# A decoder pair in three-pass float32r: the second pass of two heads' logits with 128 rows, and the lo pass of the probabilities with all 128 value columns

## The chip, the cores and the metric

The kernel runs on one core of one Trainium2 chip. A core has a matrix engine (TensorE; PE for its matmuls, PEld for its weight loads), a vector engine (DVE), a scalar engine (ACT), GpSimd (POOL) and a queue that issues most DMAs (SP). The metric is the device time of one execution in microseconds.

## The reference, cut to what matters

Two blocks over 512 tokens of width 1024. The first has two layers, each with four differential heads (two softmax maps of head dimension 64 are subtracted) and eight forgetting heads; the second has one layer with an mLSTM and an NSA mixer (eight query heads, two key groups, head dimension 64, a compressed, a selected and a window branch). With 512 tokens all eight key blocks are selected, so the selected and the window branch both work on all causal keys. The lines behind the change:

```python
# differential attention: two maps m of dimension 64 per head
logits = jnp.einsum('bqhmd,bkhmd->bhmqk', qi, k).astype(jnp.float32) * scale
p = jax.nn.softmax(logits, axis=-1)
p = p[:, :, 0] - lam * p[:, :, 1]
return jnp.einsum('bhqk,bkhe->bqhe', p.astype(v.dtype), v)
...
# NSA, selected and window branch
ls = jnp.einsum('bgrqd,bgqnd->bgrqn', qb, k_g).astype(jnp.float32) + bias_s
o_s = jnp.einsum('bgrqn,bgqnd->bgrqd', p_s, v_g.astype(jnp.float32))
```

## The kernel before

Every float32 operand x is split into hi (x rounded to float32r, by a copy) and lo = x - hi, and a product is made of three matmul passes, hi by hi, hi by lo and lo by hi (`mm3`, lines 165 to 169). Tokens lie in four tiles of 128.

For logits the head dimension is 64, half of the 128 rows of the array, so the three products are made in two passes. The query tile q holds hi of a map in one half of the partitions and lo in the other. The first pass multiplies it by a key tile that holds hi in both halves: 128 rows give hi·hi + lo·hi. The second pass takes only the 64 partitions of q that hold hi, and 64 partitions of a tile with the lo part of k: 64 rows give hi·lo. `logits` (line 551) issues both passes for each query tile i of a map m, with the first n = 128(i+1) keys as moving columns, so n is 128, 256, 384 and 512 equally often. The forgetting heads use line 551 as well, with two passes of 128 rows each, since their second tile carries the decay rows too (`fox_qk`).

For a differential head, `stacks` builds from the token-major projection a q tile (hi0, lo0, lo1, hi1, 64 columns each) and a k tile of 384 columns (hi0, hi0, lo0, lo1, hi1, hi1); `stack_T` transposes them by TensorE in groups of 128 columns (line 523, four transposes to a PSUM bank), and ACT or DVE (line 528) copies each bank to a `qk` tile. For NSA, `nsa_k` writes hi of a key group into both halves of `kn` and lo into partitions 0 to 63 (line 1518), and `nsa_soft` calls `logits`.

For the probabilities times values of forgetting and NSA heads, `pv_heads` transposes the probabilities (line 580), splits them into wh and wl, and issues for each pair of tiles a pass with the values as weights: 128 columns, hi in the first 64 and lo in the others, over wh (line 588), and a pass with the 64 hi columns over wl, into the upper 64 partitions of the sum (line 589). `fold` adds the two halves of the sum. The differential heads have their own `diff_pv`, with the weights from the probabilities.

The program interleaves a head's chain (logits, softmax, transposes, values) with matmuls of projections, gates and branches (the "feed"), which depend on weights from DMA. A scheduler with its own costs orders the instructions of each engine within these generators; the logits and stacks run under a higher priority (`hot`). PSUM has three banks with the tag A and five with the tag B; transposes and logits use B.

Of the kernel before, what the change touches and what calls it, by code (L numbers as in the profile page):

```python
# [10 lines left out]
F32 = mybir.dt.float32  # L11
F32R = mybir.dt.float32r
# [3 lines left out]
ALU = mybir.AluOpType  # L16
# [80 lines left out]
class Net:  # L97
# [410 lines left out]
        self.sub(v[:, 1:3, :], sq, v[:, 0:4:3, :])  # L508

    def k_stack(self, hl, sk):  # L510
        v = hl.rearrange("p (s d) -> p s d", d=64)
        kd = hl.rearrange("p (m c) -> p m c", c=128)[:, 0:3:2, :].rearrange("p m (e d) -> p m e d", d=64)
        self.copy(kd, sk[:, :, None, :].to_broadcast([128, 2, 2, 64]))
        self.sub(v[:, 2:4, :], sk, v[:, 0:6:5, :])

    def stack_T(self, tiles, bank='B'):

        out = []
        for which, cols in enumerate(((0, 128), (0, 256, 128))):
            for c in cols:  # L520
                p = self.pt(bank, F32R)
                for t in range(NT):
                    self.T.transpose(p[:, t * 128:(t + 1) * 128], tiles[which][t][:, c:c + 128], self.identr)  # L523
                if len(out) % 2 == 0:
                    two = self.t("qk", F32R, 1024 if len(out) < 4 else 512)
                o = two[:, len(out) % 2 * 512:len(out) % 2 * 512 + 512]
                if c == 128:
                    self.V.tensor_copy(o, p)
                else:
                    self.copy(o, p)  # L530
                out.append(o)
        q, k = out[:2], out[2:]
        return [((q[m], k[m]), (q[m][64 * m:64 * m + 64], k[2][64 * m:64 * m + 64])) for m in range(2)]

    def e_tile(self):

# [34 lines left out]
    def pv_heads(self, accs, es, val, packs, first, last):  # L571

        mm = self.T.matmul
        for pack in packs:
            p = self.pt("B")
            o, parts = 0, []
            for m, j in pack:
                n = 512 - 128 * j
                for i in range(j, NT):
                    self.T.transpose(p[:, o + (i - j) * 128:o + (i - j + 1) * 128], es[m, i][:, j * 128:(j + 1) * 128], self.ident)  # L580
                parts.append((m, j, slice(o, o + n)))
                o += n
            wh, wl = self.pair("pt")
            self.copy(wh[:, :o], p[:, :o])
            self.sub(wl[:, :o], p[:, :o], wh[:, :o])
            for m, j, c in parts:
                v, a = val(m, j), accs[m][:, j * 128:]
                mm(a, v, wh[:, c], start=first and j == 0, stop=False, skip_group_check=True)  # L588
                mm(a[0:64], v[:, 0:64], wl[:, c], start=False, stop=last and pack == packs[-1], skip_group_check=True)  # L589
            yield  # L590

    def fold(self, s, m, acc):
# [6 lines left out]
    def stage1(self, l, u):  # L599

        V = self.V
        unit = {}

        def start():
            unit["hls"] = [None] * NT, [None] * NT
            unit["rv"] = self.t("rw").rearrange("p (t m d) -> p t m d", t=NT, m=4)
            unit["vv"] = self.t("v", F32R)[:, :1024].rearrange("p (t s d) -> p t s d", t=NT, s=2)
            if u == 0:
                self.z = self.keep([128, NT, 8])

        def take(pair, ps):
            if pair == 0:
                start()
            with self.hot():
                take_hot(pair, ps)

        def take_hot(pair, ps):
            hls = unit["hls"]
            t0 = 2 * pair
            if pair == 0:  # L620
                v = self.t("hl", F32R)
                hls[0][:] = [v[:, t * 256:t * 256 + 256] for t in range(NT)]
            v = self.t("hl", F32R)
            hls[1][t0], hls[1][t0 + 1] = v[:, 0:384], v[:, 384:768]
            rv, vv = unit["rv"], unit["vv"]
            for t in (t0, t0 + 1):
                p = ps[t - t0]
                self.copy(rv[:, t], p[:, 0:256].rearrange("p (m d) -> p m d", m=4))
                self.copy(vv[:, t, 0, :], p[:, 256:384])
                self.sub(vv[:, t, 1, :], p[:, 256:384], vv[:, t, 0, :])  # L630
                if u == 0:
                    V.tensor_copy(self.z[:, t, :], p[:, 384:392])

            ts = slice(t0, t0 + 2)
            x = rv[:, ts, :, 0:16]
            ta, tb = self.t("r"), self.t("r")
            av = ta.rearrange("p (t m d) -> p t m d", t=2, m=4)
            bv = tb.rearrange("p (t m d) -> p t m d", t=2, m=4)
            cb = lambda z, lo, hi: z[:, ts, None, lo:hi].to_broadcast([128, 2, 4, hi - lo])
            V.tensor_tensor(av, x, cb(self.rc, 0, 16), op=ALU.mult)  # L640
            V.tensor_tensor(bv[:, :, :, 0:8], x[:, :, :, 8:16], cb(self.rs, 0, 8), op=ALU.mult)
            V.tensor_tensor(bv[:, :, :, 8:16], x[:, :, :, 0:8], cb(self.rs, 8, 16), op=ALU.mult)
            V.tensor_tensor(x, av, bv, op=ALU.add)
            for t in (t0, t0 + 1):
                self.stacks(hls, t, rv[:, t].rearrange("p m d -> p (m d)"))
        return take, unit
# [861 lines left out]
    def nsa_k(self, br, kv):  # L1508

        p = yield from self.dense_T(self.a["w_in_2"][0], (2824, 3080)[br])  # L1510
        b = self.bnk[:, br:br + 1]
        kv["ks"][br] = ks = []
        for g in range(2):
            own, other = slice(64 * g, 64 * g + 64), slice(64 - 64 * g, 128 - 64 * g)
            hi, lo = self.pair("kn")
            self.A(hi[own], p[own], AF.Identity, bias=b[own])
            self.A(hi[other], p[own], AF.Identity, bias=b[own])
            self.V.scalar_tensor_tensor(lo[0:64], p[own], b[own], hi[own].bitcast(F32), op0=ALU.add, op1=ALU.subtract)
            ks.append((hi, lo))
        yield  # L1520

# [60 lines left out]

    def nsa_soft(self, r, br, u, kv, es):
        hi, lo = kv["ks"][br][r // 2]
        qk = [((q, hi), (q[0:64], lo[0:64])) for q in u["q"]]
        for items in self.PACK:
            st, sc = self.t("s"), self.t("s")
            mine = [e for e, _ in self.logits(qk, items, u["bias"], rows=st)]
            n, gv = len(items), u["gv"][:, :, :, 1 + br]
            (m, i), last = items[0], items[-1]  # L1590
            g = gv[:, i, 0:2] if m != last[0] else gv[:, i:last[1] + 1:2, m] if n > 1 else gv[:, i:i + 1, m]
            self.V.reciprocal(sc[:, 0:n], st[:, 0:n])
            self.V.tensor_tensor(sc[:, 0:n], sc[:, 0:n], g, op=ALU.mult)
            for c, e in enumerate(mine):
                self.G.tensor_scalar(e, e, sc[:, c:c + 1], 0.0, op0=ALU.mult, op1=ALU.add)
                es[items[c]] = e
            yield
# [288 lines left out]
```

## Time and profile before

| | us |
|---|---|
| median of three runs | 2046.88 (2046.66 to 2047.39) |
| the profiled execution | 2052.8 |
| its span | 2050.8 |
| PE busy in it | 2007.6 (98%) |
| DVE busy | 1399.1 (68%) |
| ACT busy | 1070.7 (52%) |

The span of the profiled execution leaves out 2.0 us of that execution's time. Differential heads run at 50 to 165 us (first layer) and 650 to 770 us (second layer), NSA with the end of the mLSTM at 1420 to 1640 us. Starts of matmuls are recorded and their ends are modelled: a matmul's end lies past the start of the next, so what a matmul costs is read from start to start.

### The profile page before, as it was taken

The page shows a single profiled execution, that of the slowest core. Times are in us where ns is not written, and L with a number is a line of the kernel's source. Part 1 is how long each engine was busy: PE and PEld are TensorE (multiplying, and loading weights), DVE is VectorE, ACT ScalarE, POOL GpSimd, SP SyncE. Part 2 cuts the span into 40 slices and gives each one's busy share as a digit, 9 for nine tenths or more (in the row PEclk, how much of TensorE's full clock was granted, in tenths as well). Part 3 has the DMA queues.
Part 4 walks back from the last instruction along what each step waited for, and adds up shares of the span by engine and source line. Part 5 has one row for each costly group of instructions (what it writes and reads, how often), then busy time and mean ns, then how long its engine had stood idle before and what let it go on. Part 6 is the DMA issues. An engine that isn't in the chain of part 4 may idle for free.

```text
span 2050.8 us, 32727 instructions
## 1 busy us (share of the span) xinstructions
PE 2007.6 (98%) x12323; PEld 1770.9 (86%) x12323; DVE 1399.1 (68%) x2582; ACT 1070.7 (52%) x2129; POOL 635.2 (31%) x748
## 2 busy tenths in 40 slices
PE   8999989999999999999999999999999999999998
PEld 7988779999888988789999888888777689999987
DVE  5776778987426776778887427687665667788632
ACT  5666755554425666755554425456455535555521
POOL 0123336665201122344654201001111215565310
PEclk9999999999999999999999999999999999999999
DMA  5224242332423222342241423324221162323341
GB/s 147 73 65 121 90 161 83 124 120 78 164 78 104 74 76 78 119 136 98 87 144 62 164 84 118 110 77 124 72 73 43 51 216 73 124 83 104 113 154 52
DMA packets 198065, 211.03 MB, mean 103 GB/s; under 512 B 16263, under 2 KB 161257, under 8 KB 197907
## 3 DMA queue, kind: packets, MB, share of 16 engines
q1 hardware_dynamic: 190930, 183.24, 28.0%
q0 software_dynamic: 6976, 25.69, 3.3%
q8 instruction: 97, 1.59, 0.3%
q14 instruction: 62, 0.50, 0.1%
HBM read 196.30 MB, written 15.22 MB: 103 GB/s over the span
## 4 chain that ended last, share of the span: by engine, by line
PE 91%; DVE 3%; DMA 2%; ACT 2%; issue 1%; POOL 0%; SPq 0%; POOLq 0%; DVEq 0%; ACTq 0%
PE A L168 17%; PE A L167 17%; PE A L169 17%; PE B L168 10%; PE B L167 10%; PE B L169 10%; PE B L551 4%; PE B L580 1%; PE B L589 1%; PE B L588 1%; DMA raw<-in_w_in_dram 1%; PE B L717 1%; PE B L523 1%; DMA r<-in_w_up_dram 1%; PE B L703 0%
## 5 line engine op out<-in xcount | busy, mean ns | idle before, releaser
L163 DVE TENSOR_TENSOR lo<-raw,hi 128x1024 fp32r<-128x1024 f32 (+3 forms) x200 | 232.7, 1167 | 218.7 <-ACT hi L160 179.9
L160 ACT ACTIVATE hi<-raw 128x1024 fp32r<-128x1024 f32 (+4 forms) x208 | 204.5, 992 | 260.0 <-PE B L169 167.2
L163 DVE TENSOR_TENSOR lo<-r,hi 128x512 fp32r<-128x512 f32 (+1 forms) x240 | 269.5, 1155 | 47.3 <-ACT hi L160 42.3
L160 ACT ACTIVATE hi<-r 128x512 fp32r<-128x512 f32 (+1 forms) x240 | 193.6, 840 | 68.1 <-PE A L168 37.6
L167 PE MATMUL A<-store,hi 128*128 128x512 f32 (+1 forms) x624 | 220.0, 352 | 3.8 <-ACT hi L160 1.9
L168 PE MATMUL A<-store,hi 128*128 128x512 f32 (+1 forms) x624 | 219.3, 352 | 0.0
L169 PE MATMUL A<-store,lo 128*128 128x512 f32 (+1 forms) x624 | 218.2, 350 | 0.0
L168 PE MATMUL B<-store,hi 128*128 128x256 f32 x720 | 201.2, 279 | 0.0
L167 PE MATMUL B<-store,hi 128*128 128x256 f32 x720 | 201.2, 279 | 0.0
L169 PE MATMUL B<-store,lo 128*128 128x256 f32 x720 | 201.2, 279 | 0.0
L168 PE MATMUL A<-lo,store 128*128 128x512 f32 (+3 forms) x488 | 176.6, 363 | 0.8 <-DVE lo L163 0.8
L169 PE MATMUL A<-hi,store 128*128 128x512 f32 (+3 forms) x488 | 174.6, 361 | 2.2 <-DVE store L163 2.1
L167 PE MATMUL A<-hi,store 128*128 128x512 f32 (+3 forms) x488 | 173.2, 364 | 1.4 <-ACT store L160 1.1
L168 PEld LDWEIGHTS B<-store,hi 128*128 128x128 f32 x720 | 136.1, 189 | 0.1
L167 PEld LDWEIGHTS B<-store,hi 128*128 128x128 f32 x720 | 135.9, 189 | 0.1
L169 PEld LDWEIGHTS B<-store,lo 128*128 128x128 f32 x720 | 135.5, 188 | 0.0
L167 PEld LDWEIGHTS A<-store,hi 128*128 128x128 f32 x624 | 118.4, 190 | 19.5 <-ACT hi L160 2.4
L882 POOL TENSOR_TENSOR raw<-r,r 128x512 f32<-128x512 f32 x60 | 98.9, 1651 | 114.4 <-DMA r<-in_w_up_dram 81.4
L167 PE MATMUL A<-xs,hi 128*128 128x256 f32 x480 | 134.2, 280 | 0.0
L168 PE MATMUL A<-xs,hi 128*128 128x256 f32 x480 | 134.1, 279 | 0.0
L169 PE MATMUL A<-xs,lo 128*128 128x256 f32 x480 | 134.1, 279 | 0.0
L169 PEld LDWEIGHTS A<-store,lo 128*128 128x128 f32 x624 | 117.6, 188 | 14.4 <-issue 0.2
(427 smaller groups left out, 5572.2 us busy)
## 6 DMA issues: line engine op xcount, KB each, us to landing
r<-in_w_gate_dram SPq DMA_DIRECT2D x66, 512.0 KB, 4.5
r<-in_w_up_dram SPq DMA_DIRECT2D x66, 512.0 KB, 5.1
raw<-in_w_down_dram SPq DMA_DIRECT2D x66, 512.0 KB, 4.5
raw<-in_w_in_dram SPq DMA_DIRECT2D x64, 512.0 KB, 3.8
raw<-in_w_in_dram SPq DMA_DIRECT2D x104, 128.0 KB, 2.4
x_rows<-x POOLq DMA_DIRECT2D x20, 512.0 KB, 3.1
x<-x_rows POOLq DMA_DIRECT2D x20, 512.0 KB, 6.4
raw<-in_w_out_dram SPq DMA_DIRECT2D x28, 256.0 KB, 2.7
```

What stands on the lines that cost most here:

```text
L160: self.A(out, in_, AF.Copy, scale=scale)
L163: self.V.tensor_tensor(out, x, hi.bitcast(F32), op=ALU.subtract)
L167: mm(out, ah, bh, start=start, stop=False, skip_group_check=True)
L168: mm(out, ah, bl, start=False, stop=False, skip_group_check=True)
L169: mm(out, al, bh, start=False, stop=stop, skip_group_check=True)
L523: self.T.transpose(p[:, t * 128:(t + 1) * 128], tiles[which][t][:, c:c + 128], self.identr)
L551: self.T.matmul(pv, q[:, i * 128:(i + 1) * 128], k[:, :n], start=c == 0, stop=c == len(qk[m]) - 1, skip_group_check=True)
L580: self.T.transpose(p[:, o + (i - j) * 128:o + (i - j + 1) * 128], es[m, i][:, j * 128:(j + 1) * 128], self.ident)
L588: mm(a, v, wh[:, c], start=first and j == 0, stop=False, skip_group_check=True)
L589: mm(a[0:64], v[:, 0:64], wl[:, c], start=False, stop=last and pack == packs[-1], skip_group_check=True)
L717: mm(ov, wh[:, js], vv[:, j, :, :].rearrange("p s d -> p (s d)"), start=j == 0, stop=False, skip_group_check=True)
L882: G.tensor_tensor(s1, a21, a22, op=ALU.add)
```

## The change

`k_stack` builds a k tile of 512 columns (hi0, hi0, lo0, lo0, hi1, hi1, lo1, lo1), so that lo is there twice for each map; `stack_T` makes four groups of it instead of three. `nsa_k` writes lo into both halves. The second pass then takes the whole q tile and the whole lo tile: 128 rows, which adds lo·lo to the logits. The second pass over the probabilities takes all 128 value columns, into all 128 partitions of the sum, which adds lo·lo there.

```diff
     def k_stack(self, hl, sk):
-        v = hl.rearrange("p (s d) -> p s d", d=64)
-        kd = hl.rearrange("p (m c) -> p m c", c=128)[:, 0:3:2, :].rearrange("p m (e d) -> p m e d", d=64)
-        self.copy(kd, sk[:, :, None, :].to_broadcast([128, 2, 2, 64]))
-        self.sub(v[:, 2:4, :], sk, v[:, 0:6:5, :])
+        v = hl.rearrange("p (m z e d) -> p m z e d", m=2, z=2, d=64)
+        kk = sk[:, :, None, :].to_broadcast([128, 2, 2, 64])
+        self.copy(v[:, :, 0], kk)
+        self.sub(v[:, :, 1], kk, v[:, :, 0])
...
-        for which, cols in enumerate(((0, 128), (0, 256, 128))):
+        for which, cols in enumerate(((0, 128), (0, 256, 128, 384))):
...
-                    two = self.t("qk", F32R, 1024 if len(out) < 4 else 512)
+                    two = self.t("qk", F32R)
...
-                if c == 128:
+                if c in (128, 384):
                     self.V.tensor_copy(o, p)
...
-        return [((q[m], k[m]), (q[m][64 * m:64 * m + 64], k[2][64 * m:64 * m + 64])) for m in range(2)]
+        return [((q[m], k[m]), (q[m], k[2 + m])) for m in range(2)]
...
                 mm(a, v, wh[:, c], start=first and j == 0, stop=False, skip_group_check=True)
-                mm(a[0:64], v[:, 0:64], wl[:, c], start=False, stop=last and pack == packs[-1], skip_group_check=True)
+                mm(a, v, wl[:, c], start=False, stop=last and pack == packs[-1], skip_group_check=True)
...
-            hls[1][t0], hls[1][t0 + 1] = v[:, 0:384], v[:, 384:768]
+            hls[1][t0], hls[1][t0 + 1] = self.halves(v)
...
-            self.V.scalar_tensor_tensor(lo[0:64], p[own], b[own], hi[own].bitcast(F32), op0=ALU.add, op1=ALU.subtract)
+            for half in (own, other):
+                self.V.scalar_tensor_tensor(lo[half], p[own], b[own], hi[half].bitcast(F32), op0=ALU.add, op1=ALU.subtract)
...
-        qk = [((q, hi), (q[0:64], lo[0:64])) for q in u["q"]]
+        qk = [((q, hi), (q, lo)) for q in u["q"]]
```

The scheduler orders the instructions anew. First place: PE at the first differential head, from the last matmuls ahead of its logits. In the names, `qk_407` is the pair of q tiles, `qk_420` the two hi tiles of k, `qk_433` the lo tile (before) or the two lo tiles (after), and B_565, B_578 and so on are PSUM banks; a row with `qk_433` is a second pass. Before:

```order
L551 MATMUL B_578<-qk_420,qk_407 128x128
L551 MATMUL B_595<-qk_420,qk_407 128x384
L551 MATMUL B_595<-qk_433,qk_407 128x384
L551 MATMUL B_602<-qk_420,qk_407 128x384
L551 MATMUL B_602<-qk_433,qk_407 128x384
L551 MATMUL B_578<-qk_433,qk_407 128x128
L551 MATMUL B_623<-qk_420,qk_407 128x512
L551 MATMUL B_578<-qk_420,qk_407 128x256
L551 MATMUL B_623<-qk_433,qk_407 128x512
L551 MATMUL B_578<-qk_433,qk_407 128x256
```

And now, where B_584 is the bank of the second map that was B_578:

```order
L523 MATMUL B_435<-store_67,hl_310 128x128 x2
L523 MATMUL B_435<-store_67,hl_381 128x128 x2
L551 MATMUL B_571<-qk_420,qk_407 128x128
L551 MATMUL B_571<-qk_433,qk_407 128x128
L551 MATMUL B_571<-qk_420,qk_407 128x256
L551 MATMUL B_571<-qk_433,qk_407 128x256
L551 MATMUL B_584<-qk_420,qk_407 128x128
L551 MATMUL B_601<-qk_420,qk_407 128x384
L551 MATMUL B_601<-qk_433,qk_407 128x384
L551 MATMUL B_608<-qk_420,qk_407 128x384
L167 MATMUL A_545<-hi_464,store_67 128x384
L168 MATMUL A_545<-lo_465,store_67 128x384
```

The four transposes of the second map's lo tile (B_435) come right ahead of the logits; behind the last row shown stand 16 more projection matmuls of 384 columns, and only then the second map's second passes, with `B_608<-qk_433` first.

Second place: DVE at the same head, the copies from the transposes' banks to the `qk` tiles and what follows them. Before:

```order
L528 COPY qk_407<-B_409 128x512
L528 COPY qk_433<-B_428 128x512
L163 TENSOR_TENSOR v_518<-A_443,v_518 128x128
L640 TENSOR_TENSOR store_66<-rw_517,store_66 128x128
L641 TENSOR_TENSOR store_66<-rw_517,store_66 128x8x8
```

And now:

```order
L528 COPY qk_407<-B_409 128x512
L528 COPY qk_433<-B_428 128x512
L163 TENSOR_TENSOR v_524<-A_449,v_524 128x128
L528 COPY qk_433<-B_435 128x512
L640 TENSOR_TENSOR store_66<-rw_523,store_66 128x128
L641 TENSOR_TENSOR store_66<-rw_523,store_66 128x8x8
```

The second lo tile has a copy of its own, ahead of the rotary work of the next head and of the first softmax.

## Rows read from the trace of the kernel before

**Rows 1.** The page, busy time of PE and its share of the span:

```profile
PE 2007.6 (98%) x12323; PEld 1770.9 (86%) x12323; DVE 1399.1 (68%) x2582; ACT 1070.7 (52%) x2129; POOL 635.2 (31%) x748
```

**Rows 2.** The page, chain that ended last, by engine:

```profile
PE 91%; DVE 3%; DMA 2%; ACT 2%; issue 1%; POOL 0%; SPq 0%; POOLq 0%; DVEq 0%; ACTq 0%
```

**Rows 3.** Busy time by stage: stretch, its length, engines (instructions), PE clock, DMA:

```profile
50.00:165.00 115.00, 115.00 (x620) 97.80 (x620) 82.43 (x254) 73.20 (x201) 19.11 (x30) 1.00 0.22 61
...
1420.00:1640.00 220.00, 216.56 (x1038) 163.31 (x1037) 133.76 (x378) 114.65 (x256) 39.93 (x74) 1.00 0.19 61
```

**Rows 4.** Instructions of line 551, weight loads with two kinds of shapes (rows*columns):

```profile
L551 PEld LDWEIGHTS B<-qk,qk x128: 182/186/248, 50.5 to 770.1; 128*128 128x128 f32 x64, 64*128 64x128 f32 x64
...
L551 PEld LDWEIGHTS B<-kn,qk x128: 182/186/249, 1423.5 to 1627.9; 128*128 128x128 f32 x64, 64*128 64x128 f32 x64
```

**Rows 5.** Timeline of PE, differential head: start us, us, engine, line, tile, form:

```profile
57.44 0.82 PE L551 MATMUL B<-qk,qk 128*128 128x512 f32 x2
58.20 0.44 PE L168 MATMUL A<-lo,store 128*128 128x384 f32 x1
```

**Rows 6.** Timeline of PE, forgetting head, line 551 with two passes of 128 rows:

```profile
185.34 0.63 PE L551 MATMUL B<-hl,qk 128*128 128x512 f32 x2
185.80 0.22 PE L718 MATMUL B<-v,pt 128*128 128x128 f32 x1
...
192.69 0.44 PE L551 MATMUL B<-hl,qk 128*128 128x512 f32 x1
...
193.31 0.49 PE L703 MATMUL B<-store,ee 128*128 128x128 f32 x3
```

**Rows 7.** Timeline of PE, NSA: a pair between transposes, and four in a row:

```profile
1465.26 0.40 PE L551 MATMUL B<-kn,qk 128*128 128x512 f32 x1
...
1465.69 0.49 PE L551 MATMUL B<-kn,qk 64*128 64x512 f32 x1
1466.12 0.55 PE L580 MATMUL B<-store,ee 128*128 128x128 f32 x3
...
1494.23 1.21 PE L551 MATMUL B<-kn,qk 128*128 128x256 f32 x4
1495.38 0.39 PE L589 MATMUL B<-pt,vn 128*64 128x384 f32 x1
```

**Rows 8.** The chain that ended last, in order of time: transposes of the stacks:

```profile
71.27 0.81 PE B L523 x10
```

**Rows 9.** Timeline of PE, probabilities times values, 128 and 64 columns in turn:

```profile
1459.15 0.39 PE L588 MATMUL B<-pt,vn 128*128 128x512 f32 x1
1459.38 0.39 PE L589 MATMUL B<-pt,vn 128*64 128x512 f32 x1
1459.61 0.60 PE L580 MATMUL B<-store,ee 128*128 128x128 f32 x4
```

**Rows 10.** Groups of weight loads: busy us, mean ns of one, idle before:

```profile
L588 PEld LDWEIGHTS B<-pt,v 128*128 128x128 f32 x64 | 12.0, 188 | 9.3 <-ACT pt L160 7.9
L589 PEld LDWEIGHTS B<-pt,v 128*64 128x64 f32 x64 | 8.6, 135 | 3.6 <-DVE pt L163 2.4
```

**Rows 11.** Groups of DVE: copies of transposed stacks, subtractions, lo of NSA keys:

```profile
L528 DVE CAST qk<-B 128x512 fp32r<-128x512 f32 x16 | 10.7, 686 | 11.8 <-PE B L523 11.8
L163 DVE TENSOR_TENSOR hl<-rw,hl 128x128 fp32r<-128x128 f32 x64 | 16.1, 286 | 2.4 <-ACT hl L160 2.2
L163 DVE TENSOR_TENSOR vn<-cv,vn 128x256 fp32r<-128x256 f32 x4 | 1.7, 416 | 0.0
L1518 DVE SCALAR_TENSOR_TENSOR kn<-A,store,kn 64x512 fp32r<-64x512 f32 x4 | 3.0, 747 | 1.4 <-ACT kn L1517 1.4
```

**Rows 12.** Timeline of PE at the end of NSA, with the idle time before:

```profile
1603.76 1.21 PE L551 MATMUL B<-kn,qk 128*128 128x256 f32 x4
...
1627.02 1.32 PE L551 MATMUL B<-kn,qk 128*128 128x128 f32 x4
...
1638.05 0.96 PE L167 MATMUL A<-x,hi 128*128 128x512 f32 x3 [2.06 <-ACT x L160]
```

## The prediction

> **What bounds the kernel now.** I read the page's busy times first: PE is busy for 98% of the span [rows 1], and the chain that ended last is PE for 91% [rows 2]. An average can hide stages, so next come the stages that the change touches: in the first of the two differential stages PE is busy for all of 115 us (the second, 650 to 770 us, repeats it), in NSA for 216.6 of 220 us, while DVE stands at 82.4 of 115 us, 72%, and at 61% in NSA [rows 3]. The clock there is 1.00 throughout, the upper level of 2.4 GHz, so no time is to be had from it. The waits of PE in NSA hold one of any size, 2.06 us at the very end [rows 12]; in the two differential stages the view of PE's waits has no row at all. So these stages end when PE has worked off its list, and what PE does not do there comes off the end.
>
> But a busy PE is not a PE that streams at its peak, since ends of matmuls are modelled. I therefore read starts. Line 551 has 128 second passes with 64 rows, 64 in differential heads and 64 in NSA [rows 4], 32 of each of the four widths. In a differential head a first pass of 512 columns with 128 rows and a second one with 64 rows take from 57.44 to 58.20, 0.76 us, until the next matmul starts [rows 5]. The forgetting heads run the same line, the same two widths and the same sums with 128 rows in both passes, from 185.34 to 185.80, 0.46 us [rows 6]. The difference is 0.30 us for one second pass, and it is no wait for another engine: PE stands still on the way into the 64-row shape and again on the way out.
>
> **What the change takes away.** The same comparison at other places gives the bounds. Four NSA matmuls of 256 columns, two of them with 64 rows, take 1.15 us [rows 7]; the 1024 columns of the forgetting pair took 0.46 [rows 6]; that is 0.34 for each second pass, the upper end. Where transposes of the probabilities stand between the two passes, the NSA pair takes from 1465.26 to 1466.12, 0.86 us [rows 7], and a forgetting pair of the same width with a transpose between takes 0.62 [rows 6]: 0.24, the lower end. Transposes stand beside about a quarter of the second passes, so I take 0.29, near the clean pair. Where two second passes follow each other, as twice in the order of before shown above, the way in and out is paid once; there are nine such places, so 119 ways in and out. 119 x 0.29 = 34.5 us, with 119 x 0.24 = 28.6 and 119 x 0.34 = 40.5 as ends. About 8 us of it lie in each differential stage and 18 in NSA. A matmul of 64 rows and one of 128 stream the same columns, so the second pass itself grows by nothing.
>
> **What it adds on PE.** One more group of four transposes for each of eight differential units, 32 transposes. Ten in a row took 0.81 us [rows 8], so 32 x 0.081 = 2.6 us, all on the path, since PE has no idle time there. Between matmuls a transpose may cost more; at twice that it is 5.2.
>
> The second pass over the probabilities loads 128 columns of weights instead of 64. One load takes 188 ns instead of 135 [rows 10]. For 256 columns and more it runs beside the matmul ahead of it; for the 32 of 128 columns it does not quite fit, and I charge the whole difference: 32 x 0.053 = 1.7 us. The ends are 0 and, if none of the 128 were hidden, 6.8. Whether the change from 64 to 128 columns costs a standstill like that of the rows is read from the starts 1459.15, 1459.38 and 1459.61 [rows 9]: 0.23 us into and 0.23 out of the 64-column matmul, half of the forgetting pair's 0.46 each. So there is no standstill, and nothing is gained by dropping that shape.
>
> Sum on PE: 34.5 - 2.6 - 1.7 = 30 us less.
>
> **What it adds beside PE.** On DVE: eight copies of a bank at 0.69 us; 32 subtractions of 256 elements instead of 128, 0.42 against 0.29 us; four more lo halves of NSA keys at 0.75 us [rows 11]. That is 2.8 + 2.1 = 4.9 us in each differential stage and 3.0 in NSA. DVE then works some 87 of 107 us in the first stage, 82% instead of 72%, and 137 of 202 us in NSA, 68%: hidden by PE, which has no wait for DVE there now. If PE did wait for each of them, it would cost 12.8 us. The new order also puts in a wait: the second map's second passes wait for four transposes and a DVE copy that no other work needs. In PE's queue 18 projection matmuls of 384 columns stand ahead of them; at 0.46 x 384/1024 = 0.17 us each they cover 3.1 us, against 0.33 for the transposes and 0.69 for the copy. I cost it at nothing; without that cover each of the eight turns would cost about 1 us.
>
> What is late next: at the end of NSA, from 1603.76 to the group at 1627.02 us, 13 second passes save nearly 4 us [rows 12], but little other PE work is left there; the stage ends on logits, softmax, transposes and a wait for ACT of 2.06 us [rows 12]. I give back half, 2 us, and 1 us for short new waits in the stages, where PE now comes round sooner for what DVE and ACT make. Net 27 us less. The profiled execution took 2052.8 us, 5.9 more than the median of the runs shown; the change's part is the same in both within 0.1 us, so 2046.9 - 27 = 2020 us.
>
> **The rivals.** *DVE and ACT set the pace.* With DVE at 82% on average, bunches of copies and softmax steps may hold PE up; half of the 30 us comes back as waits: 2032 us. For it speaks that in NSA PE already waits at the end; against it that PE has no wait in the differential stages and that DVE's copies wait for PE's transposes, 11.8 us in all [rows 11].
>
> *The upper ends hold.* 0.34 us for each way in and out and no new waits: 40.5 - 4.3 = 36 us, 2011. The four NSA matmuls speak for it, the pairs between transposes against it.
>
> *The gap is not the rows.* If the 0.30 us came from a second pass as such, the change would take nothing away and its 4.3 us on PE would be added: 2051. Against it stand the forgetting heads, which have second passes and no gap. By the Trainium skill, "TensorE: Matmul & The Clock Gate", the table "Why this matters for your kernels", a single matmul of 32 rows takes the same time as one of 128, which read alone is this rival. By that rule, for the whole kernel, 2051; the trace disagrees with it for a 64-row matmul among 128-row ones, 0.76 against 0.46 us.
>
> *The columns stand still too.* If the ways into and out of the 64-column shape cost what the rows cost, hidden in both halves of that pair [rows 9], their 128 places would save another 128 x 0.29 = 37 us: 1983. The even 0.23 us speak against it. The Trainium skill, "TensorEngine Tiling (Array Packing)", "Key Properties", says that a change of tiling mode drains the engine, and lists 128 by 64 as a mode; for rows the trace agrees, for columns it shows no gap.
>
> *The turn becomes the wait* (the one that ends slower). PE runs its queue in order. If at each of the eight turns the copy of the fourth bank comes late behind DVE's queue, or its transposes wait for one of the five B banks, the second passes and all projections behind them stand. From 30/8 = 3.8 us for each turn the gain is gone; at 5 us it is 40 - 30 = 10 us more: 2057. Against it: the copy takes 0.69 us and 3.1 us of matmuls stand ahead.
>
> **How the numbers follow.** Forecast (2014 to 2026) 0.70; half comes back (2027 to 2038) 0.14; upper ends (2008 to 2013) 0.08; columns 0.02; not the rows 0.03; the turn 0.03. For 8 in 10 the range takes in the forecast, the upper ends to 2010 and the nearer part of the half: 2010 to 2033. About 0.2% (4 us) is what a measurement of this kernel can tell from no change. Faster by more than that: 0.70 + 0.14 + 0.08 + 0.02 = 0.94. Within it: a third of "not the rows", where the additions are partly hidden, and as much for a turn that just eats the gain, 0.02. Slower: 0.04.
>
> **What would show it.** Right: line 551 shows only 128 rows, a differential pair of 512 columns takes 0.46 us from start to start, four of 256 some 0.5; the differential stages are shorter by about 7 us each, NSA by 14 to 16, the rest stays. The forecast is wrong if line 551's starts still show 0.7 us and more, if PE shows waits for line 528 or for softmax that add up to over 10 us, or if a stage that has no second passes of 64 rows changes by more than a few us.

## The result and the profile after

The changed kernel takes 2014.2 us (median of 4 runs, 2006.1 to 2019.9), the kernel before on the same chip 2047.1 us (4 runs, 2046.7 to 2050.2). The ratio is 0.9833 with a 95% interval of 0.9814 to 0.9852: 33 us less. The forecast was 2020 us with 27 us less, in a range of 2010 to 2033. Direction and range hold; the saving is larger than the sum made it. In the two profiled executions the difference is larger still, 2012.6 us against 2052.8, 40.2 us; the last section says what is known of the 7 us between these two numbers.

The page of the kernel after: busy time and share of each engine, and the chain that ended last, by engine.

```profile
span 2010.7 us, 32817 instructions
...
PE 1970.4 (98%) x12355; PEld 1774.8 (88%) x12355; DVE 1396.6 (69%) x2594; ACT 1072.1 (53%) x2129; POOL 642.6 (32%) x748
...
PE 92%; DVE 3%; ACT 2%; DMA 2%; issue 1%; POOL 0%; SPq 0%; POOLq 0%; DVEq 0%; ACTq 0%
```

PE is busy for the same 98% of a span that is 40 us shorter, with 32 more instructions, the transposes [rows 1, 2]. So the share of busy time says nothing of the gain: the standstill was counted as busy time, since the ends of matmuls are modelled.

Two stages of the kernel after by windows (stretch, its length, busy time and instructions of PE, PEld, DVE, ACT and POOL, PE clock, DMA share, GB/s):

```profile
50.00:165.00 115.00, 115.00 (x677) 104.51 (x676) 93.41 (x281) 77.86 (x211) 21.70 (x32) 1.00 0.26 71
1420.00:1640.00 220.00, 216.80 (x1110) 179.56 (x1109) 151.56 (x366) 118.59 (x240) 44.24 (x84) 0.99 0.29 94
```

In the same 115 us PE starts 677 matmuls instead of 620, in NSA's 220 us 1110 instead of 1038 [rows 3]. (Work of the next stage has moved into the window, so the counts are not of the same work.) DVE stands at 81% in the differential stage, as forecast.

Line 551 of the kernel after (number of instructions: shortest, median, longest ns, first and last start, shapes as rows*columns), weight loads and matmuls, and the idle time of PE ahead of the line by what ended it:

```profile
L551 PEld LDWEIGHTS B<-qk,qk x128: 186/188/216, 49.3 to 758.4; 128*128 128x128 f32 x128
...
L551 PEld LDWEIGHTS B<-kn,qk x128: 186/188/212, 1404.5 to 1587.5; 128*128 128x128 f32 x128
L551 PE MATMUL B<-kn,qk x128: 218/340/482, 1404.6 to 1587.7; 128*128 128x512 f32 x32, 128*128 128x128 f32 x32, 128*128 128x384 f32 x32, 128*128 128x256 f32 x32
...
its engine sat idle before it (us, times) until:
...
  issue: 0.5, 1
```

All 256 loads of the changed heads have 128 rows where half had 64 [rows 4]. The last line is one that I had not read before predicting. "issue" is idle time for which the profile shows nothing that was waited for, and here it is idle time of the weight loads (PEld): for the matmuls of line 551 alone the view has no such line. It is 0.5 us once in the whole program, where the kernel before had

```profile
  issue: 20.8, 94
```

that is 94 places of 0.22 us. By the trace, 79 of the 94 stand ahead of a 64-row load behind a 128-row one and 14 ahead of a 128-row load behind a 64-row one; the last is the one that the kernel after still has. At the pair of [rows 5] it looks like this (PEld before, the idle time in brackets, and then PEld after at the pair that the next timeline shows):

```profile
57.77 0.18 PEld L551 LDWEIGHTS B<-qk,qk 64*128 64x128 f32 x1 [0.31 <-issue]
58.20 0.19 PEld L168 LDWEIGHTS A<-lo,store 128*128 128x128 f32 x1 [0.25 <-issue]
...
55.05 0.19 PEld L168 LDWEIGHTS A<-lo,store 128*128 128x128 f32 x1
55.28 0.19 PEld L169 LDWEIGHTS A<-hi,store 128*128 128x128 f32 x1
```

After, the load for line 168 starts at 55.05, 0.23 us ahead of its matmul at 55.28. Before, it starts at 58.20, together with its matmul [rows 5], and so does the 64-row load (57.77). It is so everywhere in the kernel before: at all 119 places where PE goes into the 64-row shape, and at all 119 where it comes out, the load starts within 0.003 us of its own matmul, while between two matmuls of 128 rows it starts 0.115 us ahead in the median. So where the number of rows changes, the load does not run ahead of its matmul. Whether that is the cause of the standstill or a sign of it, no run here shows.

The timeline of PE after, at the places that answer to [rows 5] and [rows 7]: start us, us, engine, line, operation, tile, shape.

```profile
54.82 0.63 PE L551 MATMUL B<-qk,qk 128*128 128x512 f32 x2
55.28 0.34 PE L168 MATMUL A<-lo,store 128*128 128x384 f32 x1
...
1584.16 0.64 PE L551 MATMUL B<-kn,qk 128*128 128x256 f32 x4
1584.63 0.34 PE L589 MATMUL B<-pt,vn 128*128 128x384 f32 x1
```

The differential pair of 512 columns takes 0.46 us instead of 0.76, and four NSA matmuls of 256 columns take 0.47 instead of 1.15: both are now what the forgetting heads took all along [rows 6].

Where the time went, from the starts of single matmuls in the two profiles (us; a stage runs from the first matmul of line 551 to the last one of its forgetting heads, NSA to the first matmul of the next feed-forward block):

| stretch | before | after | difference |
|---|---|---|---|
| first differential and forgetting stage | 189.8 | 181.9 | -7.9 |
| second | 188.1 | 180.0 | -8.1 |
| NSA to the next feed-forward block | 310.1 | 289.0 | -21.1 |
| ahead of the first stage | 50.7 | 49.3 | -1.4 |
| second feed-forward products to NSA's first line 551 | 291.3 | 289.8 | -1.5 |
| products of the first feed-forward block | 193.0 | 199.6 | +6.6 |
| products of the second | 199.6 | 193.0 | -6.6 |

The three stages hold 37 us. The two feed-forward blocks trade places; no line of theirs is changed.

### The profile page after: what moved, and what is told of

It reads as the page before. It is cut to its first block, busy times and chain, and to the rows that moved or that the text cites. A ratio compares the mean times of both kernels' runs of the same rounds, so it can differ in the third digit from the quotient of the medians.

```text
span 2010.7 us, 32817 instructions
## 1 busy us (share of the span) xinstructions
PE 1970.4 (98%) x12355; PEld 1774.8 (88%) x12355; DVE 1396.6 (69%) x2594; ACT 1072.1 (53%) x2129; POOL 642.6 (32%) x748
## 4 chain that ended last, share of the span: by engine, by line
PE 92%; DVE 3%; ACT 2%; DMA 2%; issue 1%; POOL 0%; SPq 0%; POOLq 0%; DVEq 0%; ACTq 0%
PE A L168 17%; PE A L167 17%; PE A L169 17%; PE B L169 10%; PE B L168 10%; PE B L167 10%; PE B L551 3%; PE B L580 1%; DMA r<-in_w_up_dram 1%; PE B L589 1%; PE B L523 1%; PE B L588 1%; PE B L717 1%; DVE lo L163 0%; PE B L703 0%
## 5 line engine op out<-in xcount | busy, mean ns | idle before, releaser
L883 POOL TENSOR_TENSOR r<-raw,r 128x512 f32<-128x512 f32 x60 | 98.6, 1645 | 113.8 <-DVE lo L163 106.9
```

Source lines behind the costliest of these rows:

```text
L883: G.tensor_tensor(a11, s1, a11, op=ALU.subtract)
```

## The experiments

The ratios are to the kernel before on the same chip: 2047.6 us (19 runs) for rows64, diff_only, nsa_only and pv_only, 2046.2 (15 runs) for after_again, grouped and three, 2045.4 (8 runs) for turned. "Ways" are the places at which PE comes to a 64-row second pass of line 551 from another shape, counted in the order of the trace; the kernel before has 119.

### rows64: the change with the second passes back at 64 rows

```diff
-        return [((q[m], k[m]), (q[m], k[2 + m])) for m in range(2)]
+        return [((q[m], k[m]), (q[m][64 * m:64 * m + 64], k[2 + m][64 * m:64 * m + 64])) for m in range(2)]
...
-        qk = [((q, hi), (q, lo)) for q in u["q"]]
+        qk = [((q, hi), (q[0:64], lo[0:64])) for q in u["q"]]
```

> The changed kernel with one thing undone: the second pass of the logits takes 64 partitions again (q hi and one half of the doubled lo tile); the fourth group of transposes, its copy, the doubled lo of the NSA keys and the 128 value columns stay. Theory (PE stands still on each way into and out of the 64-row shape, about 0.3 us for both): all of the gain goes and the additions stay, so 2047 + 3 = 2050 us, the first differential stage with the forgetting heads behind it about 190 us instead of 182, NSA up to the next feed-forward block about 310 instead of 289. Rival (the gain comes from the new order and from lo tiles that are made differently, not from the rows): stays near 2014 us, with 182 and 289 us.

Measured: 2053.3 us (10 runs, 2046.5 to 2062.7), ratio 1.0028 [1.0005, 1.005]. The whole gain is gone, and what the change adds is left, 6 us by the medians; by the stages the two differential ones are 2.9 and 2.3 us longer than before and NSA is 1.6 us shorter. The pair of 512 columns in its timeline (columns as above):

```profile
57.34 0.82 PE L551 MATMUL B<-qk,qk 128*128 128x512 f32 x2
58.10 0.44 PE L168 MATMUL A<-lo,store 128*128 128x384 f32 x1
```

It takes 0.76 us again, and the idle time of the weight loads ahead of line 551 is back:

```profile
  issue: 21.1, 93
```

All the additions are still in this kernel, and its 12,355 matmuls have the lines, tiles and widths of those of the kernel after, in the same order. Only the rows differ. So the rows carry the gain, and neither the order nor the new lo tiles do. Its stages are 192.7, 190.4 and 308.5 us against 181.9, 180.0 and 289.0 after: 40.8 us for 123 ways, 0.33 each.

### diff_only and nsa_only: the change in one kind of head

The first is the kernel before with the parts of the diff in the functions that build, transpose and pair the stacks (lines 510 to 533 and 624); the second has these two:

```diff
-            self.V.scalar_tensor_tensor(lo[0:64], p[own], b[own], hi[own].bitcast(F32), op0=ALU.add, op1=ALU.subtract)
+            for half in (own, other):
+                self.V.scalar_tensor_tensor(lo[half], p[own], b[own], hi[half].bitcast(F32), op0=ALU.add, op1=ALU.subtract)
...
-        qk = [((q, hi), (q[0:64], lo[0:64])) for q in u["q"]]
+        qk = [((q, hi), (q, lo)) for q in u["q"]]
```

> The kernel before with the differential part alone: k tile of 512 columns, four groups of transposes, second pass with 128 rows; NSA and the probabilities as before. Theory: the two differential stages get shorter by 8 us each as in the changed kernel (line 551 by 7.5 us each, the gaps ahead of it by 1, transposes longer by 1), NSA keeps its 310 us; about 16 us less, 2031. Rival (DVE's 4.9 us per stage and the wait for the fourth bank eat part): under 5 us for each stage, 2040.

Measured: 2026.7 us (2024.1 to 2034.5), ratio 0.9896 [0.987, 0.9922]. The differential stages are 8.2 and 8.4 us shorter, NSA 1.6 us longer. With the 1.6 us of added transposes that fall within these stages, 16.6 us net are 18.2 for 56 ways, 0.33 each.

> The kernel before with the NSA logits alone: lo of the keys in both halves, second pass with 128 rows; differential heads and probabilities as before. Theory: NSA up to the next feed-forward block goes from 310 to 289 us, the differential stages stay; about 21 us less, 2026. Rival (the end of NSA gives half back and part of the 21 us came from a luckier order): 14 us or less, 2033 or more.

Measured: 2029.0 us (2018.9 to 2032.2), ratio 0.9892 [0.9862, 0.9923]. From its first to its last matmul of line 551 and on to the next block NSA takes 287.6 us instead of 310.1: 22.5 us for 63 ways, 0.36 each. What PE waited for in NSA of this kernel (engine, line, releaser: us in total, times, longest):

```profile
PE A L167 <- ACT x L160: 2.1, 1, 2.1
PE B L1499 <- issue: 0.9, 1, 0.9
PE B L588 <- ACT pt L160: 0.5, 1, 0.5
PE B L580 <- POOL ee L1596: 0.5, 2, 0.3
PE B L1625 <- ACT wc L160: 0.3, 1, 0.3
PE B L589 <- DVE pt L163: 0.3, 1, 0.3
```

The wait at the very end was there before [rows 12]; the others come to 2.5 us, against 22.5 saved. In the stages that they change, the two halves save 16.6 + 22.5 = 39 us, of which the kernel after keeps 37 together with the 128-column pass. They are not quite separate: the differential stages, which were expected to stay, are 1.5 us longer each in nsa_only, as NSA is by 1.6 in diff_only and by 1.7 in pv_only. These kernels have new orders, so a change of 1 to 2 us in a single stage need not come from the rows.

### pv_only: the probabilities' lo part with 128 columns, alone

```diff
-                mm(a[0:64], v[:, 0:64], wl[:, c], start=False, stop=last and pack == packs[-1], skip_group_check=True)
+                mm(a, v, wl[:, c], start=False, stop=last and pack == packs[-1], skip_group_check=True)
```

> The kernel before with the lo pass of the probabilities alone: 128 value columns instead of 64. Theory (columns cost no standstill; only the longer weight load shows, where the matmul has 128 columns): 0.7 to 1.7 us more in all, 2048; line 589 up by some 0.02 us per matmul on average. Rival (a change of columns stands still as a change of rows does): some 0.29 us less for each of 128 places, 37 us less, 2010.

Measured: 2045.1 us (10 runs, 2040.0 to 2054.2), ratio 0.9993 [0.9973, 1.0014]: no difference, and the 0.7 to 1.7 us that were expected are too small for this ratio to show. Counted by starts, line 589 takes 1.4 us more in all, 0.9 of it in NSA. The timeline of PE in NSA, wide and narrow:

```profile
1457.34 0.40 PE L588 MATMUL B<-pt,vn 128*128 128x512 f32 x1
1457.58 0.39 PE L589 MATMUL B<-pt,vn 128*128 128x512 f32 x1
1457.81 0.27 PE L580 MATMUL B<-store,ee 128*128 128x128 f32 x1
```

0.24 and 0.23 us from start to start with 128 columns, 0.23 and 0.23 with 64 [rows 9]. A shape of fewer columns costs no standstill here; the rival of 1983 us falls.

### after_again: the kernel after once more

It is the changed kernel, run again to tell 33 us from 40.

> The changed kernel again, unaltered, to see how single executions of it and of the kernel before are spread. Theory: the stages of the change save 40 us in every execution (differential 8 + 8, NSA 21, rest), and what differs between executions is the pace of the 256-column matmuls in the first two feed-forward blocks, 113 or 118 ns, 7 us for a block; so the medians of many runs on one chip differ by 37 to 41 us (some 2008 against 2047), ratio 0.980 to 0.982. Rival (the change itself costs the feed-forward blocks time, and 33 us is what it is worth): a median of 2013 to 2015, ratio 0.983 to 0.985, and slow blocks in most profiles.

Measured: 2009.0 us (5 runs, 2003.5 to 2015.1), ratio 0.9828 [0.9805, 0.985], 37 us less. That is in agreement with the stages, but the interval of the ratio touches both expectations, so the ratio alone does not decide. The profile speaks against the rival: the stages are 181.9, 180.0 and 290.2 us, 36 us shorter than before, and slow blocks in most profiles, the rival's condition, are not there. Here the first block turned slow only near 455 us and the second stayed fast; in the first profile of this kernel the first block was slow and the second fast. Two profiles are few.

### grouped: both first passes of a group ahead of both second passes

The kernel before, with the loops of line 551 exchanged:

```diff
-            for c, (q, k) in enumerate(qk[m]):
-                self.T.matmul(pv, q[:, i * 128:(i + 1) * 128], k[:, :n], start=c == 0, stop=c == len(qk[m]) - 1, skip_group_check=True)
...
+        for c in range(2):
+            for _, pv, m, i in out:
+                q, k = qk[m][c]
+                self.T.matmul(pv, q[:, i * 128:(i + 1) * 128], k[:, :128 * (i + 1)], start=c == 0, stop=c == 1, skip_group_check=True)
```

This kernel does not compute what the reference does: where two logits share a bank, their two sums are interleaved in it, and the result is another. How that comes about no run here shows. The matmuls are the same in number, shape and operands.

> The kernel before, rows and all, with one thing altered: in a group of two logits both first passes are issued ahead of both second passes. The work is the same, but second passes of 64 rows can follow each other. Theory (the price is paid for each way into and out of the shape, not for each matmul): with 20 to 30 ways fewer, 6 to 9 us less, most in NSA (5 of it), about 2040; line 551 with its neighbours shorter by 0.3 us for each way that goes. Rival (each 64-row matmul costs 0.3 us by itself): no change beyond 2 us.

Measured: 2038.8 us (10 runs, 2033.7 to 2041.5), ratio 0.996 [0.9947, 0.9974], 7.4 us less. The order has 94 ways, 25 fewer: 0.30 each. No second pass has gone and none has more rows; only their neighbours have changed.

### turned: the passes of every second logit the other way round

The kernel before, with the order 128, 64, 64, 128 rows within a group in place of 128, 64, 128, 64; the sums are those of the reference.

```diff
-            for c, (q, k) in enumerate(qk[m]):
+            for c, (q, k) in enumerate(qk[m][::-1] if o and qk[m][1][0].shape[0] == 64 else qk[m]):
```

> The kernel before, with its 64-row second passes, where in a group of two logits the second one has its passes turned round: first 128 rows, then 64; then 64, then 128. No work is added or left out, and the sums are the same. Theory (a price for each way into and out of the shape): the two 64-row passes of a group stand side by side, some 25 to 35 ways fewer than 119, so 7 to 11 us less: about 2038, ratio 0.9945 to 0.9965. Rival (each 64-row matmul costs 0.3 us by itself): within 2 us of before, ratio 0.999 to 1.001.

Measured: 2037.5 us (5 runs, 2035.6 to 2039.2), ratio 0.9957 [0.9942, 0.9972]. 93 ways, 26 fewer: 7.9 us by the medians, 0.30 each. The stages are 1.1, 1.2 and 5.9 us shorter, 8.2 us, 0.31 each. The timeline of PE in NSA, a group of four and a single pair:

```profile
1484.82 1.02 PE L551 MATMUL B<-kn,qk 128*128 128x256 f32 x4
1485.68 0.34 PE L589 MATMUL B<-pt,vn 128*64 128x384 f32 x1
...
1486.94 0.83 PE L551 MATMUL B<-kn,qk 128*128 128x512 f32 x2
1487.70 0.66 PE L580 MATMUL B<-store,ee 128*128 128x128 f32 x4
```

Four of 256 columns with two 64-row passes side by side take 0.86 us: 1.15 when they stand apart [rows 7], 0.47 when no pass has 64 rows. The single pair, which has no neighbour to share with, still takes 0.76. Two 64-row matmuls in a row pay once, 0.39 us here with the matmul behind them inside the stretch. So the cost belongs to the change of shape and not to the 64-row matmul as such.

### three: fewer additions for the same rows

If only the rows matter, the fourth bank of the differential heads isn't needed. This kernel keeps the three transposed groups of the kernel before, whose third holds the lo parts of both maps' keys above each other, and uses all its 128 rows for either map; NSA is as in the kernel after, line 589 as before. Against the kernel after:

```diff
-        for which, cols in enumerate(((0, 128), (0, 256, 128, 384))):
+        for which, cols in enumerate(((0, 128), (0, 256, 128))):
...
-        return [((q[m], k[m]), (q[m], k[2 + m])) for m in range(2)]
+        return [((q[m], k[m]), (q[m], k[2])) for m in range(2)]
...
-                mm(a, v, wl[:, c], start=False, stop=last and pack == packs[-1], skip_group_check=True)
+                mm(a[0:64], v[:, 0:64], wl[:, c], start=False, stop=last and pack == packs[-1], skip_group_check=True)
```

The added half multiplies the lo part of a map's queries with the lo part of the other map's keys, a product of two lo parts that the reference does not have; the kernel after adds that of its own keys there, and the kernel before neither.

> 128 rows without the extra work: NSA as in the changed kernel, but for differential heads the k tile of 384 columns and three groups as before, where the second pass takes the whole q tile (hi and lo of one map) over the whole lo tile (lo of both maps), so that a product of lo by lo of the other map is added in place of the map's own; the probabilities' lo pass keeps its 64 columns. Theory: line 551 as in the changed kernel, 32 transposes fewer (2.2 us less on PE), the shorter weight load back (0.8 us less): 3 us below the changed kernel, ratio to before 0.979 to 0.981; first differential stage with the forgetting heads behind it 180.5 us instead of 182. Rival (the standstill comes back wherever the two halves of a tile hold different maps, or the fourth group cost nothing): differential stage 190 us, or no difference to the changed kernel.

Measured: 2000.3 us (5 runs, 1999.1 to 2001.4), ratio 0.9785 [0.9768, 0.9802], 46 us less than before and faster than both kernels: 8.7 us below after_again on the same chip, where 3 were expected. Its stages are 179.8, 178.2 and 287.7 us, 5.3 us less than those of the kernel after: 1.6 from line 523, 1.2 from line 589, 1.2 from line 551, the rest spread over the projections. Against the profile of after_again (spans of 1997.4 and 2006.9 us) the stages hold 6.4 us, the pace of the first block 1.5, and the stretches from the forgetting heads to the first two blocks 4.5, while 2.7 go back between the second block and NSA. Why those stretches differ is open. The matmuls of its first differential stage have the shapes of the kernel after:

```profile
L551 PE MATMUL B<-qk,qk x64: 218/334/477, 48.0 to 146.8; 128*128 128x128 f32 x16, 128*128 128x256 f32 x16, 128*128 128x384 f32 x16, 128*128 128x512 f32 x16
```

## Why the prediction was right, and where its sum was too small

**What bounds the kernel.** Right: what PE does not do came off the end. The three stages became 37 us shorter, and the chain is still PE's.

**The gap is the rows.** Right, and shown from three sides: rows64 takes the whole gain away by the rows alone, turned and grouped take a fifth to a quarter of it by order alone, and the pair fell from 0.76 to 0.46 us. The rival of 2051 falls. The Trainium skill, "TensorE: Matmul & The Clock Gate", the table "Why this matters for your kernels", gives a single matmul of 32 rows the time of one of 128; for 64 rows among 128 the runs show some 0.3 us beside it for every way in and out. The Trainium skill, "TensorEngine Tiling (Array Packing)", "Key Properties", says that a change of tiling mode drains the engine: for rows the runs agree, for columns (pv_only) they show no gap.

**0.29 us for a way in and out.** This term was mis-sized. The runs give 0.30 to 0.31 (turned, grouped), 0.33 (rows64, diff_only) and 0.36 (nsa_only). The last has 2.1 us of line 588 in it, which became 1.5 to 2.1 us shorter in NSA in rows64, diff_only and pv_only too, where NSA's second passes still have 64 rows, so that goes with the new order; without it nsa_only gives 0.32. For 119 ways 0.30 to 0.33 are 36 to 39 us instead of 34.5.

The step that failed is where the windows of [rows 5] and [rows 7] end: at the start of the matmul behind the second pass. That matmul is held up as well. In the timeline of PE it takes until the next start, before and then after:

```profile
58.20 0.44 PE L168 MATMUL A<-lo,store 128*128 128x384 f32 x1
58.48 0.34 PE L169 MATMUL A<-hi,store 128*128 128x384 f32 x1
...
55.28 0.34 PE L168 MATMUL A<-lo,store 128*128 128x384 f32 x1
55.46 0.34 PE L169 MATMUL A<-hi,store 128*128 128x384 f32 x1
```

0.28 us against 0.18: 0.10 us that the clean pair's 0.30 does not hold. Four in a row have the matmul behind the first of their second passes inside the window, and gave 0.34; so the upper end was nearer. Counted from start to start over all 119 ways, against the medians of the same line and width in the kernel after, the cost is 14 us on the matmuls ahead, 19 on the second passes and 5 on matmuls behind that do not themselves stand ahead of one: 38 us, 0.32 each. That is less than this pair's 0.40, since a matmul between two ways is counted once, and beside transposes a way costs less: a pair of 512 columns with one transpose between takes 0.63 us in the kernel after (1439.13 to 1439.76), and took 0.86 [rows 7]. Line 551 itself saved 31.2 us of it, 0.26 for each way; the rest lies with its neighbours. In NSA 18 us were forecast for the ways; the stage shows 21 to 22.5, some 2 of it line 588's.

**The additions.** The 32 transposes cost 2.2 us (2.6 forecast). Line 589's longer loads cost 0.8 in the kernel after and 1.4 alone (1.7 forecast). The work beside PE is hidden: over the first differential stage, 49 to 160 us, and over the second, 650 to 780 us, the view of PE's waits has no row at all, so that 4.9 us more of DVE in each and the turns cost nothing. The rivals of DVE and ACT, and of the turn, fall.

**What was given back.** 2 us at the end of NSA and 1 us of new waits were not. The tail of the kernel after in PE's timeline (in brackets the idle time ahead and what ended it), and all that PE waited for from 1400 to 1600 us:

```profile
1587.20 0.84 PE L551 MATMUL B<-kn,qk 128*128 128x128 f32 x4
...
1597.88 0.96 PE L167 MATMUL A<-x,hi 128*128 128x512 f32 x3 [2.06 <-ACT x L160]
```

```profile
PE A L167 <- ACT x L160: 2.1, 1, 2.1
PE B L588 <- ACT pt L160: 0.5, 1, 0.5
PE B L589 <- DVE pt L163: 0.3, 1, 0.3
PE B L580 <- POOL ee L1596: 0.2, 1, 0.2
```

From the last group of line 551 to the next stage 10.7 us pass, before 11.0 [rows 12], with the same 2.06 us for ACT. Everything ahead of that group came forward with it, softmax and transposes too, so nothing was late there. The short waits are 1.0 us; before, they were 1.4.

Together: 36 to 39 us for the ways, less 3.0 for the additions, is 33 to 36; the stages show 37, with some 2 us of line 588 in them that the order gave. The forecast's 34.5 - 4.3 - 3 was short by about 4 in the first term, by 1 and 3 in the others, and had no term for the order. By its own signs the differential stages were to be shorter by about 7 us and NSA by 14 to 16; they are by 8 and 21. One sign of being wrong did show, a stage without 64-row passes that changed by more than a few us: both feed-forward blocks, by 6.6 us each way, which the last section takes up. That the measured 33 us lies nearer to 27 than to 37 is luck, as far as can be told: after_again measured 37.

## What to carry to other kernels

Where PE sets the end, count how often its matmuls go from one number of rows to another: each way in and out took 0.30 to 0.33 us here, while a pass with its unused rows filled took no longer, and making the second lo tile took 2.2 us of transposes, which three shows can be saved. If the rows can't be filled, stand the narrow matmuls next to each other; a change of order alone took 8 us off. Read the cost from start to start, beginning at the matmul ahead of the narrow one and ending behind the one that follows it, and look at the idle time that the weight loads show under "issue".

## What the runs showed that I had not expected

**Two paces of the same feed-forward block.** The 256-column matmuls of a block run for most of it either at 113.3 or at 117.8 ns from start to start, with the same program lines and a granted clock of 1.00 both ways. Three windows of 100 us, one in each block, line 167's instructions alone (busy time and instructions of PE and PEld, clock, DMA share, GB/s). The kernel before:

```profile
340.00:440.00 100.00, 80.37 (x295) 55.08 (x294) 1.00 0.35 119
960.00:1060.00 100.00, 78.87 (x284) 53.67 (x283) 1.00 0.31 101
1760.00:1860.00 100.00, 78.87 (x284) 53.67 (x283) 1.00 0.34 112
```

and the kernel after:

```profile
340.00:440.00 100.00, 78.86 (x283) 53.16 (x284) 1.00 0.33 106
960.00:1060.00 100.00, 80.43 (x296) 55.19 (x295) 1.00 0.29 94
1760.00:1860.00 100.00, 78.66 (x283) 53.51 (x284) 1.00 0.29 96
```

295 or 284 of them in the same 100 us: 4% of a block, 193.0 against 199.6 us for its products. Nothing ties it to the change. In the ten profiles the third block is slow every time, the first is slow from its start only in the profile of the kernel after and the second only in that of the kernel before, and in two profiles (grouped, after_again) the first block turned slow on the way, near 455 us. The rate of the DMA doesn't go with it (119 and 101 GB/s in before, 106 and 94 in after, the faster block once with more, once with less). What chooses the pace is open; I have tried nothing on it.

A block that turns is worth up to 6.6 us, and the four runs of the changed kernel are spread by twice that (2006.1, 2012.6, 2015.8, 2019.9). With it, the 33 us of the medians and the 40 of the profiles can both hold beside 37 in the stages, but I could read the paces only in the profiled runs, so that for the medians this is argued, not shown. It also means that a few runs do not resolve 0.2% of this kernel, as the prediction took for granted: rows64's interval is 0.0045 wide with 10 runs against 19.

**The columns cost nothing.** With 512 columns streamed, 64 and 128 columns of weights take the same time between starts (0.23 us), although the rows, the other side of the same array, stop the engine for 0.3 us.
